# 64 batched 128x128 matrix products: row pairs of a and out packed on 64 partitions

## Chip, cores, metric

One core of one Trainium2 chip. The metric is the device time of one execution in microseconds; lower is better. For this kernel a run is called slow when it is over 1.5% above the fastest of the same kernel; verdicts use the other runs, called fast.

## The reference

```
a, b: (64, 128, 128) float32
out = np.matmul(a, b)              # (64, 128, 128) float32
```

## The kernel before

The first 8 matrices come in as float32 on two hardware queues and are cast by VectorE. All others are cast to float16 while they are loaded, by transfers that GpSimd issues, and the float16 results are cast back to float32 while they are stored, on the same GpSimd queue. TensorE transposes a (against an identity), VectorE copies the transposed block to SBUF, TensorE multiplies, ScalarE evicts.

```
a0f = sb.tile([P, G, P], F32)                  # P = 128, G = 8
nc.sync.dma_start(out=a0f[:, 0:4], in_=a[0:4].rearrange("b m k -> m b k"))
nc.sync.dma_start(out=a0f[:, 4:8], in_=a[4:8].rearrange("b m k -> m b k"))
...                                            # b0f likewise, on the scalar queue
in_chunks = [(8, 16), (16, 32), (32, 48), (48, 64)]
for (lo, hi) in in_chunks:
    sl = ds(lo, hi - lo)
    nc.gpsimd.dma_start(out=a16[:, sl], in_=a[sl].rearrange("b m k -> m b k"))
    nc.gpsimd.dma_start(out=b16[:, sl], in_=b[sl].rearrange("b k n -> k b n"))
...
for g in range(n_groups):                      # 8 groups of 8 matrices
    ...
        nc.tensor.transpose(aT_ps[:, j], a16[:, i], ident)
    nc.vector.tensor_copy(out=aT16[:, gs], in_=aT_ps)
    ...
        nc.tensor.matmul(c_ps[:, j], aT16[:, i], b16[:, i], start=True, stop=True)
    nc.scalar.copy(out=c16[:, gs], in_=c_ps)
    nc.gpsimd.dma_start(out=out[gs].rearrange("b m n -> m b n"), in_=c16[:, gs])
```

## Time and profile before

| | before |
|---|---|
| time, median of 20 runs (range) | 41.75 us (41.54 to 42.31) |
| span of the profiled execution | 40.0 us |
| DMA packets | 24,929 |
| matmul instructions on TensorE | 128 |

A span is shorter than a time by some 1.8 us (41.73 and 40.0 us in the profiled run before, 41.42 and 39.5 after), which lie outside the profile. The prediction reads the steady stretches. Two further places matter for what came of it. The first is the list of DMA queues of the page (packets, MB, time taken as a share of 16 engines' span):

```profile
q0 software_dynamic: 22816, 7.90, 176.9%
q10 hardware_dynamic: 1056, 0.52, 5.0%
q1 hardware_dynamic: 1056, 0.52, 4.7%
q8 instruction: 1, 0.02, 0.1%
```

q0 is GpSimd's queue, q1 and q10 carry the first 8 matrices of a and of b. The last line is one transfer of 16 KB of instructions (the trace has it at 25.1 us, 0.94 us long). The second place is the DMA view of the kernel before from 4 to 5 us, where the first loads are under way and GpSimd's queue has only just begun:

```profile
DMA packets 622, 0.32 MB, mean 318 GB/s; under 512 B 17, under 2 KB 617, under 8 KB 622
q1 hardware_dynamic: 407, 0.20, 73.5%
q10 hardware_dynamic: 207, 0.10, 41.3%
q0 software_dynamic: 8, 0.01, 3.7%
```

At 22.35 ns a row, 622 packets are 13.9 of the 16 us of engine time that this microsecond offers: nearly full.

### The profile page before, as it was taken

The page shows a single profiled execution, that of the slowest core. Times are in us where ns is not written, and L with a number is a line of the kernel's source. Part 1 is how long each engine was busy: PE and PEld are TensorE (multiplying, and loading weights), DVE is VectorE, ACT ScalarE, POOL GpSimd, SP SyncE. Part 2 cuts the span into 40 slices and gives each one's busy share as a digit, 9 for nine tenths or more (in the row PEclk, how much of TensorE's full clock was granted, in tenths as well). Part 3 has the DMA queues.
Part 4 walks back from the last instruction along what each step waited for, and adds up shares of the span by engine and source line. Part 5 has one row for each costly group of instructions (what it writes and reads, how often), then busy time and mean ns, then how long its engine had stood idle before and what let it go on. Part 6 is the DMA issues. An engine that isn't in the chain of part 4 may idle for free.

```text
span 40.0 us, 357 instructions
## 1 busy us (share of the span) xinstructions
PE 12.6 (31%) x128; PEld 10.7 (27%) x128; DVE 7.3 (18%) x12; ACT 9.1 (23%) x9; POOL 16.8 (42%) x21
## 2 busy tenths in 40 slices
PE   0000005085499935007998309004600000000000
PEld 0000013092496904007968208004400000000000
DVE  0000444608400480000076003900000000000000
ACT  0191000000049500900090980000891000000000
POOL 2799999999801780062006279000057400000000
PEclk9999999999999999995557999999655555555555
DMA  0079999999999999999999999999999999999900
GB/s 0 13 210 341 319 247 184 180 179 184 182 180 184 183 180 183 184 179 183 183 181 182 181 182 182 213 362 374 367 365 368 364 363 369 366 360 369 140 9 0
DMA packets 24929, 8.96 MB, mean 224 GB/s; under 512 B 14672, under 2 KB 24912, under 8 KB 24928
## 3 DMA queue, kind: packets, MB, share of 16 engines
q0 software_dynamic: 22816, 7.90, 176.9%
q10 hardware_dynamic: 1056, 0.52, 5.0%
q1 hardware_dynamic: 1056, 0.52, 4.7%
q8 instruction: 1, 0.02, 0.1%
HBM read 8.42 MB, written 4.19 MB: 316 GB/s over the span
## 4 chain that ended last, share of the span: by engine, by line
POOL 38%; issue 36%; POOLq 3%
POOL out_dram L78 15%; POOL a_70 L55 11%; POOL b_71 L56 10%; POOLq L106 2%; POOL ident L50 2%; POOLq L78 0%; POOLq L95 0%
## 5 line engine op out<-in xcount | busy, mean ns | idle before, releaser
L78 POOL DMA_DIRECT2D out_dram<-c_73 x8 | 7.0, 881 | 13.6 <-ACT c_73 L77 13.1
L77 ACT CAST c_73<-c_ps 128x1024 f16<-128x1024 f32 x8 | 7.8, 1014 | 19.1 <-PE c_ps L74 19.1
L70 PE MATMUL aT_ps<-ident,a_70 128*128 128x128 f16 x64 | 7.1, 288 | 11.4 <-DMA ident<-ident_const 6.5
L70 PEld LDWEIGHTS <-a_70 128*128 128x128 f16 x64 | 5.8, 132 | 12.1 <-DMA a_70<-in_a_dram 5.8
L71 DVE COPY aT_72<-aT_ps 128x1024 f16<-128x1024 f16 x8 | 5.3, 689 | 13.0 <-PE aT_ps L70 13.0
L74 PE MATMUL c_ps<-b_71,aT_72 128*128 128x128 f16 x64 | 5.9, 260 | 4.7 <-DMA b_71<-in_b_dram 3.7
L74 PEld LDWEIGHTS <-aT_72 128*128 128x128 f16 x64 | 4.9, 118 | 5.6 <-DVE aT_72 L71 3.0
L56 POOL DMA_DIRECT2D b_71<-in_b_dram x4 | 4.6, 1150 | 0.0
L55 POOL DMA_DIRECT2D a_70<-in_a_dram x4 | 4.5, 1113 | 0.0
L77 ACT ACT_TABLE_LOAD x1 | 1.3, 1283 | 1.8 <-issue 1.8
L58 DVE CAST a_70<-a0f 128x512 f16<-128x512 f32 x1 | 0.6, 561 | 4.5 <-DMA a0f<-in_a_dram 4.5
L50 POOL DMA_DIRECT2D ident<-ident_const x1 | 0.7, 703 | 0.8 <-POOLq L95 0.8
L61 DVE CAST b_71<-b0f 128x512 f16<-128x512 f32 x1 | 0.6, 634 | 0.4 <-DMA b0f<-in_b_dram 0.4
L59 DVE CAST a_70<-a0f 128x512 f16<-128x512 f32 x1 | 0.4, 426 | 0.8 <-DMA a0f<-in_a_dram 0.8
L60 DVE CAST b_71<-b0f 128x512 f16<-128x512 f32 x1 | 0.4, 407 | 0.0
L95 POOL MEMSET const-float32-0.0<- 128x1 f32 x1 | 0.1, 98 | 0.2 <-issue 0.2
L95 POOL MEMSET const-bfloat16-1.0<- 128x1 bf16 x1 | 0.1, 101 | 0.0
L95 POOL MEMSET const-float32-1.0<- 128x1 f32 x1 | 0.1, 98 | 0.0
L95 POOL MEMSET const-uint8-127<- 128x1 uint8 x1 | 0.1, 98 | 0.0
## 6 DMA issues: line engine op xcount, KB each, us to landing
out_dram<-c_73 POOLq DMA_DIRECT2D x8, 512.0 KB, 11.8
a_70<-in_a_dram POOLq DMA_DIRECT2D x3, 512.0 KB, 12.0
b_71<-in_b_dram POOLq DMA_DIRECT2D x3, 512.0 KB, 13.6
b0f<-in_b_dram ACTq DMA_DIRECT2D x2, 256.0 KB, 5.0
a0f<-in_a_dram SPq DMA_DIRECT2D x2, 256.0 KB, 4.4
a_70<-in_a_dram POOLq DMA_DIRECT2D x1, 256.0 KB, 6.1
b_71<-in_b_dram POOLq DMA_DIRECT2D x1, 256.0 KB, 6.7
ident<-ident_const POOLq DMA_DIRECT2D x1, 32.0 KB, 5.2
```

What stands on the lines that cost most here:

```text
L50: nc.gpsimd.dma_start(out=ident, in_=ident_dram.ap())
L55: nc.gpsimd.dma_start(out=a16[:, sl], in_=a[sl].rearrange("b m k -> m b k"))
L56: nc.gpsimd.dma_start(out=b16[:, sl], in_=b[sl].rearrange("b k n -> k b n"))
L58: nc.vector.tensor_copy(out=a16[:, 0:4], in_=a0f[:, 0:4])
L59: nc.vector.tensor_copy(out=a16[:, 4:8], in_=a0f[:, 4:8])
L61: nc.vector.tensor_copy(out=b16[:, 4:8], in_=b0f[:, 4:8])
L70: nc.tensor.transpose(aT_ps[:, j], a16[:, i], ident)
L71: nc.vector.tensor_copy(out=aT16[:, gs], in_=aT_ps)
L74: nc.tensor.matmul(c_ps[:, j], aT16[:, i], b16[:, i], start=True, stop=True)
L77: nc.scalar.copy(out=c16[:, gs], in_=c_ps)
L78: nc.gpsimd.dma_start(out=out[gs].rearrange("b m n -> m b n"), in_=c16[:, gs])
L106: with _tile.TileContext(nc) as tc:
```

## The change

A matrix of a is read as 64 rows of 1 KiB, two neighbouring rows of 512 B each, and lies on 64 partitions; out is stored in the same form. So there are fewer, longer contiguous runs. b stays as it was, since its rows are the contraction. TensorE pays with twice the instructions (256 for 128), ScalarE with 16 evictions on 64 partitions (1010 ns each in the trace after) for 8 on 128 (1014 ns). The split of the loads is changed as well.

```
-    a0f = sb.tile([P, G, P], F32)
+    Fa0f = sb.tile([H, G, 2 * P], F32)                     # H = 64
...
-    nc.sync.dma_start(out=a0f[:, 0:4], in_=a[0:4].rearrange("b m k -> m b k"))
-    nc.sync.dma_start(out=a0f[:, 4:8], in_=a[4:8].rearrange("b m k -> m b k"))
+    nc.sync.dma_start(
+        out=Fa0f, in_=a[0:G].rearrange("b (q two) k -> q b (two k)", two=2)
+    )
...
-    in_chunks = [(8, 16), (16, 32), (32, 48), (48, 64)]
+    in_chunks = [(8, 24), (24, 40), (40, 56), (56, 64)]
...
-            nc.tensor.transpose(aT_ps[:, j], a16[:, i], ident)
+            for e in range(2):
+                nc.tensor.transpose(
+                    aT_ps[:, j, ds(H * e, H)], Fa[:, i, ds(P * e, P)], id64
+                )
...
+        for h in range(G // HG):                            # HG = 4
+            h0 = g0 + h * HG
+            c_ps = ps_c.tile([H, HG, 2 * P], F32)
+            for j in range(HG):
+                i = h0 + j
+                for e in range(2):
+                    nc.tensor.matmul(c_ps[:, j, ds(P * e, P)],
+                        aT16[:, i, ds(H * e, H)], b16[:, i], start=True, stop=True)
+            nc.scalar.copy(out=c16[:, ds(h0, HG)], in_=c_ps)
         nc.gpsimd.dma_start(
-            out=out[gs].rearrange("b m n -> m b n"), in_=c16[:, gs]
+            out=out[gs].rearrange("b (q two) n -> q b (two n)", two=2),
+            in_=c16[:, gs],
         )
```

More of the change, by code (lines that the diff above doesn't have):

```diff
@@ L22 @@
     P = 128
+    H = 64
     B = a.shape[0]
@@ L27 @@
     G = 8
+    HG = 4
     n_groups = B // G
@@ L35 @@
     ident = consts.tile([P, P], F16)
-    a0f = sb.tile([P, G, P], F32)
+    Fa0f = sb.tile([H, G, 2 * P], F32)
     b0f = sb.tile([P, G, P], F32)
-    a16 = sb.tile([P, B, P], F16)
+    Fa = sb.tile([H, B, 2 * P], F16)
     b16 = sb.tile([P, B, P], F16)
     aT16 = sb.tile([P, B, P], F16)
-    c16 = sb.tile([P, B, P], F16)
-    nc.sync.dma_start(out=a0f[:, 0:4], in_=a[0:4].rearrange("b m k -> m b k"))
-    nc.sync.dma_start(out=a0f[:, 4:8], in_=a[4:8].rearrange("b m k -> m b k"))
+    c16 = sb.tile([H, B, 2 * P], F16)
+    nc.sync.dma_start(
+        out=Fa0f, in_=a[0:G].rearrange("b (q two) k -> q b (two k)", two=2)
+    )
     nc.scalar.dma_start(out=b0f[:, 0:4], in_=b[0:4].rearrange("b k n -> k b n"))
@@ L50 @@
     nc.gpsimd.dma_start(out=ident, in_=ident_dram.ap())
-    in_chunks = [(8, 16), (16, 32), (32, 48), (48, 64)]
+    in_chunks = [(8, 24), (24, 40), (40, 56), (56, 64)]
     for (lo, hi) in in_chunks:
         sl = ds(lo, hi - lo)
-        nc.gpsimd.dma_start(out=a16[:, sl], in_=a[sl].rearrange("b m k -> m b k"))
+        nc.gpsimd.dma_start(
+            out=Fa[:, sl],
+            in_=a[sl].rearrange("b (q two) k -> q b (two k)", two=2),
+        )
         nc.gpsimd.dma_start(out=b16[:, sl], in_=b[sl].rearrange("b k n -> k b n"))
-    nc.vector.tensor_copy(out=a16[:, 0:4], in_=a0f[:, 0:4])
-    nc.vector.tensor_copy(out=a16[:, 4:8], in_=a0f[:, 4:8])
+    nc.vector.tensor_copy(out=Fa[:, 0:G], in_=Fa0f)
     nc.vector.tensor_copy(out=b16[:, 0:4], in_=b0f[:, 0:4])
     nc.vector.tensor_copy(out=b16[:, 4:8], in_=b0f[:, 4:8])
+    id64 = ident[0:H, 0:H]
     for g in range(n_groups):
@@ L66 @@
         aT_ps = ps_t.tile([P, G, P], F16)
-        c_ps = ps_c.tile([P, G, P], F32)
         for j in range(G):
             i = g0 + j
-            nc.tensor.transpose(aT_ps[:, j], a16[:, i], ident)
+            for e in range(2):
+                nc.tensor.transpose(
+                    aT_ps[:, j, ds(H * e, H)], Fa[:, i, ds(P * e, P)], id64
+                )
         nc.vector.tensor_copy(out=aT16[:, gs], in_=aT_ps)
-        for j in range(G):
-            i = g0 + j
-            nc.tensor.matmul(
-                c_ps[:, j], aT16[:, i], b16[:, i], start=True, stop=True
-            )
-        nc.scalar.copy(out=c16[:, gs], in_=c_ps)
+        for h in range(G // HG):
[4 more added lines that the diff above has]
+                for e in range(2):
+                    nc.tensor.matmul(
+                        c_ps[:, j, ds(P * e, P)],
+                        aT16[:, i, ds(H * e, H)],
+                        b16[:, i],
+                        start=True,
+                        stop=True,
+                    )
+            nc.scalar.copy(out=c16[:, ds(h0, HG)], in_=c_ps)
         nc.gpsimd.dma_start(
-            out=out[gs].rearrange("b m n -> m b n"), in_=c16[:, gs]
+            out=out[gs].rearrange("b (q two) n -> q b (two n)", two=2),
+            in_=c16[:, gs],
         )
```

## The prediction

> **What bounds the kernel now.** I read the slices of the page first, because the share of the span of each engine is low (PE 31%, ScalarE 23%, VectorE 18%, GpSimd 42%), so none of them is a candidate over the whole.
>
> ```profile
> DMA  0079999999999999999999999999999999999900
> GB/s 0 13 210 341 319 247 184 180 179 184 182 180 184 183 180 183 184 179 183 183 181 182 181 182 182 213 362 374 367 365 368 364 363 369 366 360 369 140 9 0
> DMA packets 24929, 8.96 MB, mean 224 GB/s; under 512 B 14672, under 2 KB 24912, under 8 KB 24928
> ```
>
> A slice is 1.0 us. The 16 DMA engines are at nine tenths from slice 3 to slice 37 without a hole. The rate has two flat levels: about 182 GB/s while inputs are loaded, about 365 GB/s while outputs are stored. That is one level, not two: the size counted is that of the destination. A load reads 512 B of float32 and writes 256 B of float16, a store reads 256 B and writes 512 B. Next I took the DMA view in one stretch of each kind, 10 to 24 us and 27 to 36 us.
>
> ```profile
> DMA packets 10028, 2.55 MB, mean 182 GB/s; under 512 B 10028, under 2 KB 10028, under 8 KB 10028
> ```
>
> ```profile
> DMA packets 6542, 3.29 MB, mean 366 GB/s; under 512 B 108, under 2 KB 6542, under 8 KB 6542
> ```
>
> Loads: 14 us x 16 engines / 10028 packets = 22.3 ns of an engine per packet. Stores: 9 us x 16 / (6542 - 108 small ones) = 22.4 ns. The same time per packet in both directions, whatever side is the float32 one: an engine needs 22.35 ns for a 512 B row, and the kernel is a queue of such rows. Check by adding up: the GpSimd queue carries 56 matrices of a, 56 of b and 64 of c, each 128 rows, 176 x 128 / 16 = 1408 rows per engine, x 22.35 ns = 31.5 us. By the same view its packets start in earnest at 5 us (8 in the slice 4 to 5, 232 in 5 to 6, where the first loads on the other two queues are ending) and end at about 37.3 us. 5.5 + 31.5 = 37.0. So it fits, with no idle in it.
>
> Then the end. The chain of waits follows only GpSimd's issuing and is no help here; the waits of the DMA queue's own engine, SyncE, tell what the end waits for, and the timeline tells when the last stores were queued.
>
> ```profile
> SPq L106 <- DMA out_dram<-c_73: 36.9, 4, 32.8
> ```
>
> ```profile
> 27.47 0.92 PEld L74 LDWEIGHTS <-aT_72 128*128 128x128 f16 x16 [2.58 <-issue]
> 27.50 1.16 PE L74 MATMUL c_ps<-b_71,aT_72 128*128 128x128 f16 x16 [2.44 <-DMA b_71<-in_b_dram]
> 28.14 1.93 ACT L77 CAST c_73<-c_ps 128x1024 f16<-128x1024 f32 x2 [4.27 <-PE c_ps L74]
> 29.45 0.88 POOL L78 DMA_DIRECT2D out_dram<-c_73  x1 [4.41 <-ACT c_73 L77]
> 30.56 0.88 POOL L78 DMA_DIRECT2D out_dram<-c_73  x1 [0.23 <-issue]
> ```
>
> All loads are queued ahead of all stores, so stores start to flow only when the loads end, at 25.6 us (slice 25 is the step in the rate). By then six stores are queued, which last 6 x 64 rows x 22.35 ns = 8.6 us, to 34.2 us. The last store is queued at 31.4 us. Compute is 2.8 us early: it is hidden.
>
> [...]
>
> **The change part by part.**
> *Rows of 1 KiB.* a and out become 64 rows of 1 KiB per matrix; b stays at 512 B. On the GpSimd queue: a 56 x 64 / 16 = 224 rows per engine, out 256, in all 480 rows of 1 KiB in place of 960 of 512 B; b 448 as before. A pair of old rows costs 44.7 ns[...]. I take 1.35 us. All of it is on the path, as the queue has no hole. A page count of about 16,700 packets should result (24,929 - 512 x 16).
> [...]What crosses the SBUF side is float16, half the bytes. [...]I deduct 0.25 us for queueing. Only the first load of a is float32 in SBUF[...]. It runs beside b's first load before the GpSimd queue starts, where the slices 2 to 5 have room (410, 697, 622 and 582 packets against 716 in a full one), so I deduct 0.2 us and not 1.0.
> *TensorE.* 64 transposes and 64 matmuls become 128 and 128. In the timeline 16 of either kind took 1.89 us[...], 1.07 to 1.19 us[...]. 256 instructions: 17 to 19 us, or 30 us. [...] Per group of 8 matrices that is 2.1 to 3.8 us, while loads bring a group in [...]2.8 us. [...] A slow PE may fall behind the loads, but up to the end of the loads it needs only 4 or 5 of the 8 stores ready[...].
> *ScalarE.* 16 evictions of 64x1024 in place of 8 of 128x1024; [...]16 x 1.014 = 16.2 us instead of 7.8. Per group 2.0 us, under the 2.8 us of its loads. *VectorE.* The eight 689 ns copies stay; two casts of a (561 + 426 ns) become one of 64x2048, an estimated 1.2 to 1.6 us by four times the 407 ns of the fastest 512-element one. Off the path.
> *GpSimd.* An issue of 1024 rows takes 0.88 us, of 2048 rows 1.14 to 1.38; 512 rows will take an estimated 0.75. Off the path.
> *Chunks.* (8,24), (24,40), (40,56), (56,64): the last chunk is one group instead of two. After the last b lands, one group is left: 16 matmuls and two evictions, about 2.5 us, as now. The smaller first chunk is lost, at no cost while the queue is full.
> Sum: 1.35 - 0.25 - 0.2 = 0.9 to 1.1 us. 41.79 - 1.1 = 40.7 us.
>
> **The rivals.**
> *A[...].* [...]a row costs more than 44.7 ns. Every ns over that costs 0.48 us. At 48 ns: 43.4 us. [...]
> *B: HBM or bytes bound, not rows.* If 366 GB/s is a byte rate, longer rows do nothing: 41.8 us. For it: loads and stores have the same rate[...]. [...]
> *C: compute turns into the bound.* PE [...]leaves the last stores late. If the last group is done 3 us later than now, at 34.4 us, then the data ends [...]37.3 us: the gain is gone, 41.8 us. For it: the PE count doubles[...]. Against it: 2.8 us of slack now.
>
> **Range and chances.** The main line (40.0 to 40.9 us) gets about half. It is only a little over the 2% line, 40.95 us, so small losses [...]lead to "same", 0.30. Rival A in earnest or C strongly: 0.18 for slower. Range: full gain without deductions and a little luck in the start gives 39.6; a row at 47 ns or a lagging PE gives 43.0.
>
> **What would show it.** Right: some 16,700 packets; in the load stretches alternating rates (a faster than 182 GB/s[...], b at 182); [...]the step from loads to stores near 25 us instead of 25.6; no hole in the DMA row; the last store queued before the DMA has drained the rest. Wrong by A: stores and a's loads below 366 and 182 GB/s. Wrong by B: the same 366 with half the packets. Wrong by C: holes in the DMA row after 25 us, or the last store queued later than about 33.5 us. Also wrong if the start moves: the GpSimd queue begins later than 5 us or the first a lands over 1 us later and group 0 starts late.

The trace before has no row of 1 KiB and no tile on 64 partitions. So the gain of 1.35 us, the 0.25 us, the 0.2 us and the 1.0 us of the first load were the author's estimates and not measured. Rival A is that rows of 1 KiB on 64 partitions cost more than the 44.7 ns of two old ones.

## The result

| | before | after |
|---|---|---|
| median of all runs | 41.75 us (20 runs) | 41.66 us (10 runs; 41.13 to 42.99) |
| ratio of the fast runs | 1 | 0.9902, interval 0.9865 to 0.9938 |
| span of the profiled execution | 40.0 us | 39.5 us |
| DMA packets | 24,929 | 16,722 |

A ratio here and below is the mean time of one kernel's fast runs over that of the other's of the same rounds, so not quite the ratio of the medians. The change gives 1%, 0.41 us of 41.75, where 40.7 us, 1.1 us less, was predicted. With the profiled one, 5 of the changed kernel's 11 runs are slow, at 41.75 to 42.99 us; nothing below is concluded from those.

The slices and queues of the page after:

```profile
DMA  0089999999999999999999999999999999999200
GB/s 0 15 247 283 206 224 223 199 199 181 183 183 196 199 189 183 183 187 199 208 179 182 183 192 188 187 378 397 400 404 403 377 386 403 397 395 299 45 1 0
DMA packets 16722, 8.98 MB, mean 227 GB/s; under 512 B 7488, under 2 KB 16704, under 8 KB 16720
...
q0 software_dynamic: 15136, 7.90, 134.1%
q1 hardware_dynamic: 528, 0.52, 6.1%
q10 hardware_dynamic: 1056, 0.52, 5.8%
q8 instruction: 2, 0.03, 0.3%
```

Three things are to be seen. The rates rose as hoped: a's loads run at 196 to 199 GB/s (slices 7, 8, 12, 13, 18), b's still at 183, the stores at about 400 instead of 365. The start got worse: in slices 3 to 6 the rate is 283, 206, 224, 223, where before it was 341, 319, 247, 184. (The last of before is low because GpSimd's casting loads, which count at 256 B of the 512 B they read, already filled it.) And there are two transfers of instructions instead of one.

The DMA view after, for 12 to 14 us (loads of a) and 27 to 36 us (stores):

```profile
DMA packets 786, 0.40 MB, mean 198 GB/s; under 512 B 17, under 2 KB 786, under 8 KB 786
```

```profile
DMA packets 3573, 3.57 MB, mean 396 GB/s; under 512 B 106, under 2 KB 3572, under 8 KB 3572
```

2 us x 16 / (786 - 17) = 41.6 ns for a 1 KiB row in the loads, 9 us x 16 / (3573 - 106) = 41.5 ns in the stores, the latter with a 16 KB transfer of instructions among them. A pair of old rows took 44.7. So the gain per row is there, in both directions, 3.2 ns: 1.5 us over 480 rows, where the prediction took 1.35. With it the loads of a group come to the 2.8 us of the prediction, 8 x (4 x 41.5 + 8 x 22.35) ns.

The DMA view after from 4 to 5 us, to be held against that of before above:

```profile
DMA packets 230, 0.20 MB, mean 205 GB/s; under 512 B 2, under 2 KB 230, under 8 KB 230
q1 hardware_dynamic: 174, 0.18, 95.1%
q10 hardware_dynamic: 56, 0.03, 17.8%
```

At full rate 174 long rows x 41.5 ns and 56 short ones x 22.35 ns would be 8.5 us of engine time, of 16: with work queued the engines do about half of what they could. A packet of q1 took 87 ns on average (95.1% of 16 us / 174). From 3.5 to 4.5 us, where q1 is almost alone, 201 of its rows start: 206 GB/s. In the half microsecond before, 160 rows of q1 start, 328 GB/s. So this load on partitions 0 to 63 begins fast and then falls to about 206; why is not shown. GpSimd's queue, which had 232 packets in the slice 5 to 6 us before, has 1 there now and 263 in the next.

The last work of the changed kernel in its timeline:

```profile
30.68 0.61 PE L87 MATMUL c_ps<-b_71,aT_72 128*64 128x128 f16 x8 [0.30 <-ACT c_73 L94]
...
30.93 0.69 POOL L95 DMA_DIRECT2D out_dram<-c_73  x1 [1.11 <-ACT c_73 L94]
32.74 0.70 POOL L95 DMA_DIRECT2D out_dram<-c_73  x1 [1.14 <-ACT c_73 L94]
```

The last store is queued at 33.4 us instead of 31.4. The DMA row stays at nine tenths until slice 36, so in this execution compute did not hold the stores, but its lead is mostly used up: the data of the seven stores before it lasted until 35.1 us, 1.6 us longer; by the same measure the lead was 4.4 in the kernel before (35.9 and 31.4).

**Which engine ends last.** GpSimd's queue has 272 packets of 4 bytes for its 17 transfers, so 16 for each, and I take it that every DMA engine ends its share with one of them (the trace does not say which engine a packet is on). Taking these packets in order of time, 16 to a transfer, gives when the median engine and when the late ones were done with it. From the packets of before and after, us (the rows of loads and early stores thinned out):

```
before   median engine done         20.1  23.0  25.9  27.3  30.1  33.0  35.9  37.3
         last engine later by       0.60  0.60  1.09  1.11  1.11  1.11  1.11  1.11
         second last later by       0.42  0.42  0.60  0.60  0.60  0.60  0.60  0.60
         instructions at            25.1
after    median engine done         17.5  20.2  24.4  27.2  29.8  31.1  33.8  36.4
         last engine later by       0.13  1.06  1.06  0.99  1.01  1.03  1.03  1.26
         second last later by       0.13  0.13  0.13  0.13  0.16  0.98  0.98  1.03
         instructions at            19.2, 30.2
```

After each transfer of instructions one engine is some 0.9 us late at once, and in these two traces the lag stays to the end (1.09 to 1.11 us before, 1.06 to 1.26 after). In before the engine that it hit became the last, beside one that was 0.6 us late from the start. So the profiled pair adds up: median engine 37.32 to 36.40 (-0.92), last engine over the median 1.11 to 1.26 (+0.15), last packet to end of span 1.52 to 1.88 (+0.36): -0.41 us in all, the spans' difference. Of two transfers of instructions, then, the last engine shows only 0.15 more than of one.

### The profile page after: what moved, and what is told of

It is laid out like the page before. It is cut to its first block, busy times and chain, and to the rows that moved or that the text cites. A ratio compares the mean times of both kernels' runs of the same rounds, so it can differ in the third digit from the quotient of the medians.

```text
span 39.5 us, 616 instructions
## 1 busy us (share of the span) xinstructions
PE 18.2 (46%) x256; PEld 15.6 (40%) x256; DVE 7.7 (19%) x11; ACT 16.4 (42%) x17; POOL 15.1 (38%) x21
## 2 busy tenths in 40 slices
DMA packets 16722, 8.98 MB, mean 227 GB/s; under 512 B 7488, under 2 KB 16704, under 8 KB 16720
## 4 chain that ended last, share of the span: by engine, by line
issue 46%; POOL 35%; POOLq 2%
POOL out_dram L95 12%; POOL Fa L58 11%; POOL b_71 L62 10%; POOLq L124 2%; POOL ident L53 2%; POOLq L95 0%; POOLq L113 0%
## 5 line engine op out<-in xcount | busy, mean ns | idle before, releaser
L94 ACT CAST c_73<-c_ps 64x1024 f16<-64x1024 f32 x16 | 15.1, 1010 | 14.3 <-PE c_ps L87 14.3
L77 PE MATMUL aT_ps<-ident,Fa 64*128 64x64 f16 x128 | 7.4, 220 | 11.7 <-DVE Fa L64 9.5
L87 PE MATMUL c_ps<-b_71,aT_72 128*64 128x128 f16 x128 | 11.7, 250 | 1.4 <-ACT c_73 L94 1.4
L95 POOL DMA_DIRECT2D out_dram<-c_73 x8 | 5.6, 697 | 17.3 <-ACT c_73 L94 17.3
L77 PEld LDWEIGHTS <-Fa 64*128 64x128 f16 x128 | 6.1, 114 | 12.8 <-DVE Fa L64 9.5
L87 PEld LDWEIGHTS <-aT_72 128*64 128x64 f16 x128 | 9.6, 129 | 2.7 <-issue 2.0
L58 POOL DMA_DIRECT2D Fa<-in_a_dram x4 | 4.4, 1102 | 0.0
L64 DVE CAST Fa<-Fa0f 64x2048 f16<-64x2048 f32 x1 | 1.2, 1203 | 0.0
```

Source lines behind the costliest of these rows:

```text
L58: nc.gpsimd.dma_start(out=Fa[:, sl], in_=a[sl].rearrange("b (q two) k -> q b (two k)", two=2),)
L64: nc.vector.tensor_copy(out=Fa[:, 0:G], in_=Fa0f)
L77: nc.tensor.transpose(aT_ps[:, j, ds(H * e, H)], Fa[:, i, ds(P * e, P)], id64)
L87: nc.tensor.matmul(c_ps[:, j, ds(P * e, P)], aT16[:, i, ds(H * e, H)], b16[:, i], start=True, stop=True,)
L94: nc.scalar.copy(out=c16[:, ds(h0, HG)], in_=c_ps)
L95: nc.gpsimd.dma_start(out=out[gs].rearrange("b (q two) n -> q b (two n)", two=2), in_=c16[:, gs],)
```

## The experiments

All were correct unless said otherwise, and were timed in 5 rounds beside the kernel before on the same chip. Theory P: rows gain as predicted, the float32 load of the first 8 matrices loses on partitions 0 to 63. Theory F: the second transfer of instructions costs too. Rival C: compute holds the stores.

### 1. Undo the start (e1_after_start128)

```
-    Fa0f ... one load of a[0:8] on 64 partitions, 1 KiB rows
+    nc.sync.dma_start(out=a0f[:, 0:4], in_=a[0:4].rearrange("b m k -> m b k"))
+    nc.sync.dma_start(out=a0f[:, 4:8], in_=a[4:8].rearrange("b m k -> m b k"))
...
+            if g == 0:
+                nc.tensor.transpose(aT_ps[:, j], a016[:, i], ident)
...
-                        aT16[:, i, ds(H * e, H)],
+                        aT16[:, i, ds(e, H, step=2)] if g == 0 else aT16[:, i, ds(H * e, H)],
```

> The changed kernel with one part undone: the first 8 matrices of a are loaded as before (two transfers, rows of 512 B, float32 on all 128 partitions); everything else stays packed. Theory P (the changed kernel's start loses about 1 us[...]): the GpSimd queue's packets start near 5.0 us again instead of 6.0, the step from loads to stores moves from 25.7 to about 24.8 us, and the time falls from 41.4 (fast runs of the changed kernel) to about 40.6, ratio to before 0.97. Rival C (compute, that is ScalarE's 16 evictions and the doubled TensorE work, holds the end): the start moves but the last stores are not queued earlier than 32.7 us, holes appear in the stores, and the time stays at 41.2 to 41.5. Rival Q (the GpSimd queue starts late because of its own issues or chunks): the start stays at 6.0 and the time at 41.4.

Measured: ratio 0.9731 (0.9661 to 0.98; 3 of 6 runs fast, 40.37 to 40.84). Undoing the start gains (0.9902 - 0.9731) x 41.75 = 0.7 us. The profiled run is a slow one; only its start is read here, its rates by slice:

```profile
GB/s 0 12 198 332 331 255 191 198 185 180 183 192 198 193 185 183 184 195 199 201 176 183 189 191 183 338 388 395 403 401 395 408 373 390 397 322 74 31 1 0
```

332, 331, 255 in slices 3 to 5: the start of before is back, and the step to the stores comes in slice 25 instead of 26. Theory P expected this; rival Q (GpSimd's own issues or chunks delay its queue) falls, as those are unchanged here.

### 2. The start alone, in short rows (e2_before_start64)

```
+    for e in range(2):
+        nc.sync.dma_start(
+            out=Fa0f[:, e], in_=a[0:G, ds(H * e, H)].rearrange("b q k -> q b k")
+        )
...                                             # group 0: two transposes of 64 rows per matrix
```

> The kernel before with one part of the change alone: the first 8 matrices of a are loaded onto 64 partitions, but in rows of 512 B (rows q and 64 + q instead of pairs of neighbours) and in two transfers. Theory P[...]: the GpSimd queue starts about 0.9 us later than the 5.0 of before, and the time is about 42.6, ratio 1.02, although no row became longer and no transfer was merged. Rival L (the long rows or the single transfer make the late start): start at 5.0 and the time at 41.75.

Measured: ratio 1.0155 (1.0103 to 1.0208), all 6 runs fast: +0.65 us, with rows of 512 B and two transfers as before. So neither the row length nor the merging is needed for a loss; the expected 0.9 was somewhat too much. In its trace the median engine is done with the first GpSimd load at 7.60 us instead of 7.16 and with the last store at 37.83 instead of 37.32; the last engine is 1.48 us late instead of 1.11. So 0.4 to 0.5 us come from the start and the rest from a late engine.

### 3. The merged transfer alone (e7_before_one_dma)

```
+    nc.sync.dma_start(out=a0f, in_=a[0:8].rearrange("b m k -> m b k"))     # in place of two
```

> The kernel before with the first two transfers of a merged to one of 512 KB on 128 partitions, and one cast in place of two. Theory P: start of the GpSimd queue near 5.0, time 41.75, ratio 1.00. Rival L (one transfer instead of two makes the late start): start near 6.0, time 42.6, ratio 1.02.

Measured: 1.0021 (0.9996 to 1.0047). One transfer instead of two costs nothing to speak of.

### 4. 64 other partitions (e11_start64_all_ports)

```
-    Fa0f[:, e]                                  # partitions 0 to 63
+    Fa0f[ds(32, H), e]                          # partitions 32 to 95; cast in pieces of 32
```

> As e2 (the kernel before, first 8 matrices of a on 64 partitions in float32), but on partitions 32 to 95 instead of 0 to 63[...]. Theory P[...]: the loss of e2 goes; GpSimd queue in earnest at 5 to 5.5 us, 41.8, ratio 1.00. Rival N (it is the number of partitions[...]): as e2, 42.4, ratio 1.0155.

Measured: 1.0083 (1.0048 to 1.0118), all 14 runs fast. The DMA view from 3 to 4 us, first of e2, then of this run:

```profile
DMA packets 542, 0.27 MB, mean 271 GB/s; under 512 B 16, under 2 KB 541, under 8 KB 542
```

```profile
DMA packets 696, 0.34 MB, mean 342 GB/s; under 512 B 28, under 2 KB 696, under 8 KB 696
```

The same 64 partitions' worth of data moves at 342 GB/s instead of 271, as in the kernel before (697 packets, 342 GB/s). The line of a's queue in this run, in the same microsecond:

```profile
q1 hardware_dynamic: 518, 0.26, 85.8%
```

Without the 16 small ones that is 257 GB/s into 64 partitions, b's rows beside it. So the rate in the start depends on which 64 partitions are written and not on their number alone; why is not shown. Here too a's first packet comes only at 2.86 us, as in e2 (2.66) and in the changed kernel (2.78; before 1.82), and the first GpSimd load is done at 7.28 us all the same, so that delay is not the cause. The time gives back only 0.3 of the 0.65 us, though: the median engine ends at 37.5 (before 37.3, e2 37.8), but two engines end at 38.75 and 38.98, one late from the start by 1.2 us, the other after the transfer of instructions at 29.0. The expectation of a ratio of 1.00 was missed for this; why an engine is late from the start is open.

### 5. The same rows on 128 partitions (e4_pairs128)

Two neighbouring matrices are 128 row pairs in one piece of memory, so one row pair can go to each of 128 partitions, and a transpose is full-sized again. The two halves of the partitions are the two matrices; each matmul writes the half of PSUM that belongs to its matrix.

```
+    def rows(x):
+        return x.rearrange("(t h) m k -> t (h m) k", h=2).rearrange(
+            "t (p two) k -> p t (two k)", two=2)
...
+        for t in range(G // 2):
+            for e in range(2):
+                nc.tensor.transpose(aT_ps[:, 2*t + e], a16[:, g0//2 + t, ds(P*e, P)], ident)
...
+                    nc.tensor.matmul(c_ps[ds(H*h, H), t, ds(P*e, P)],      # for t, h, e
+                        aT16[:, g0 + 2*t + e, ds(H*h, H)], b16[:, g0 + 2*t + h],
+                        start=True, stop=True)
...
+        nc.gpsimd.dma_start(out=rows(out[gs]), in_=c16[:, ds(g0//2, G//2)])
```

> Another packing with the same 1 KiB rows, on all 128 partitions: one row pair of two neighbouring matrices per partition, so 64 full transposes as before, 128 matmuls of 64 columns whose outputs go to the lower or upper half of the partitions, and 8 evictions of 128 x 1024. Theory P with the row cost (41 ns per 1 KiB against 44.7 for two of 512 B, on 480 rows per engine): rates of 198 and 400 as in the changed kernel, start near 5.0, step near 24.7, time 41.75 - 1.7 = 40.0 to 40.3, ratio 0.96 to 0.965. Rival C (compute holds the changed kernel): same start as e1, but better than e1 by more than 0.4 us. Rival H[...]: a rate above 198 and 400 here.

Measured: 40.28 us, ratio 0.9643 (0.9597 to 0.9689), all 6 runs fast. It is the version that beats both kernels clearly. Its slices:

```profile
DMA  0169999999999999999999999999999999999400
GB/s 0 17 159 336 367 284 174 198 187 183 183 189 197 199 185 183 183 192 198 194 185 183 196 187 186 221 351 401 402 398 401 399 396 395 396 398 307 84 0 0
```

198 in a's loads and 400 in the stores, no more than the changed kernel has on 64 partitions. So rival H, that 64 partitions slow the float16 rows as well, falls at these rates. The start is whole (336, 367, 284). From 4 to 5 us the same 1 KiB float32 rows of a, on 128 partitions, took 44 ns a packet (63.2% of 16 us / 229) where the changed kernel's took 87:

```profile
q1 hardware_dynamic: 229, 0.22, 63.2%
```

The 4-byte packets show the two kernels side by side: the median engine is done with the first GpSimd load of a at 9.10 us in the changed kernel and at 8.20 here, with the last load at 25.85 and 24.97, with the last store at 36.40 and 35.48. The distance is 0.90, 0.88 and 0.92: all of it is there after the start, and nothing is added in 27 us of float16 rows on 64 partitions. The other profiles agree on the first of these times: 9.0 to 9.3 us in the three with the changed kernel's start, 8.2 to 8.4 in the five with long rows and a's first load on all partitions. The last engine is 1.26 us late in the changed kernel and 1.19 here, with a single transfer of instructions.

### 6. Loads alone and stores alone (e13_pairs_loads_only, e14_pairs_stores_only)

```
# loads alone: rows back in order in VectorE's copy, the rest as before
+        nc.vector.tensor_copy(
+            out=aT16[:, gs].rearrange("p (t h) (q e) -> p t (h q) e", h=2, e=2),
+            in_=aT_ps.rearrange("p t e x -> p t x e"))
# stores alone: a as before, output as in 5
+                        aT16[:, i, ds(e, H, step=2)],
```

> The 128-partition packing for the loads of a alone; VectorE's copy out of PSUM puts the rows back in order, and matmuls, evictions and stores are as in the kernel before. 224 rows of 1 KiB per engine x 3.5 ns = 0.78 us less; a rate of 198 in a's loads, 366 in the stores. If the 0.36 us that all kernels with 1 KiB stores lose between the last completion packet and the end belong to the stores, this kernel does not have them: 1.5 to 1.6 us from last packet to end as before, and the time near 41.0, ratio 0.981. If they belong to the packed loads or to the count of TensorE instructions: about 1.88 and ratio near 0.99.

> The 128-partition packing for the stores alone; a is loaded as before, and the matmul takes every second column of the transposed a. 256 rows per engine x 3.5 = 0.90 us less in the stores (400 instead of 366), loads at 182. If the longer end belongs to the 1 KiB stores: 1.88 us from the last packet to the end, so a net 0.54 us, ratio about 0.987. If not: 1.5 to 1.6 us and ratio about 0.979.

Measured: 0.9818 (0.9777 to 0.986) and 0.9767 (0.9736 to 0.9798): -0.76 us for 224 rows per engine and -0.97 us for 256, by the 3.5 ns a row of the expectations, an estimate of the author's, 0.78 and 0.90, by the 3.2 of the trace after 0.72 and 0.82. The gain per row is confirmed by time as well. Both together (run 5) give 1.49, not 1.73. Part of the rest is at the end, which SyncE's waits show, for the kernel before, the changed kernel, loads alone and stores alone:

```profile
SPq L106 <- PEq L106: 0.8, 2, 0.5
```

```profile
SPq L124 <- PEq L124: 1.2, 2, 0.7
```

```profile
SPq L118 <- PEq L118: 0.9, 2, 0.5
```

```profile
SPq L117 <- PEq L117: 1.0, 2, 0.5
```

These are the waits at the closing barrier, after all data has landed. From the last packet to the end it is 1.52, 1.88, 1.61 and 1.69 us, 1.90 in run 5, 1.86 to 1.89 in the other kernels with long rows both ways and 1.51 to 1.62 in those without long rows. Neither half has the 0.36 us alone, so what I asked of these two runs stays unanswered: what makes the closing barrier longer is open. The count of TensorE instructions alone does not (e6 in the next section, 256 pairs: 1.55).

### 7. More instructions on TensorE (e6_before_more_pe, e10_pairs_more_pe)

```
+            for _ in range(3):                  # before; range(2) in the kernel of run 5
                 nc.tensor.transpose(...)
```

> The kernel before with every transpose done three times over (result unchanged): 256 pairs of weight load and matmul, as many as the changed kernel has. Theory F (a second 16 KB transfer of instructions costs the changed kernel part of its gain): two such transfers in the trace, two engines about 1 us late or one 2 us late, and a time 0 to 0.3 us longer with some executions 1 us longer, as the changed kernel has. Rival: nothing but noise, 41.75, no slow executions. A rise above 0.5 us in all executions would speak for TensorE's work itself holding the end.

> The 1 KiB packing on 128 partitions (e4) with every transpose done twice: 256 pairs on TensorE as in the changed kernel, so two 16 KB transfers of instructions instead of one; result and all else unchanged. Theory F (the second transfer is what e1 still lacks against e4): 40.5 to 40.7, near e1's ratio of 0.973, with some slow executions near 41.5. Rival C (the 16 evictions are what e1 lacks): 40.3 as e4.

Measured: 1.0056 (1.0026 to 1.0085; 22 runs) for the first, +0.23 us; 0.9737 (0.967 to 0.9804; 5 of 6 runs fast) for the second against 0.9643 in run 5, +0.39 us. The last queue line of run 5 and of this run:

```profile
q8 instruction: 1, 0.02, 0.2%
```

```profile
q8 instruction: 2, 0.03, 0.3%
```

The first lies in the expected 0 to 0.3 us; the executions 1 us longer did not come (the longest of 22 took 42.71). All six profiles with 248 or more pairs on TensorE have two such transfers, those with 192 or fewer have one (e3's comes after its end). By the same completion packets as above, the lag in e6's trace jumps from 0.45 to 1.5 us after the transfer at 17.0 and the second engine's from 0.37 to 1.18 after the one at 30.1; in e10's from 0.35 to 0.95 after 18.4 and the second's from 0.31 to 0.85 after 30.2. The stores have no hole. At the end the last engine of e6 is 1.46 us late against 1.11 before, which fits theory F and its time. e10 fits less well: its last engine is 1.27 us late, but run 5 had one 1.19 late with a single transfer, and the median engine is 0.18 us slower (35.66 against 35.48), so most of the 0.26 us between their last packets is not this lag. By time, what e1 lacks against run 5 (0.9731 against 0.9643) comes back in e10 with 8 evictions of 128 partitions, so rival C's 16 evictions are not needed for it. But the intervals of e1 and of e10 both overlap that of run 5, the plain mean of e10's five fast runs (40.85 us) would make it 0.55 instead of 0.39, and the repeated transposes are TensorE work as well. Theory F is shown in e6, at 0.23 us with that reserve; for the changed kernel its size stays open.

### 8. Fewer matmuls (e5_before_fewer_pe, e9_after_fewer_pe)

```
# before, wrong on purpose: 32 matmuls of 256 columns
+            nc.tensor.matmul(c_ps[:, ds(j, 2)], aT16[:, i], b16[:, ds(i, 2)], ...)   # even j
# after, wrong on purpose: 64 matmuls of 256 columns
+                nc.tensor.matmul(c_ps[:, j], aT16[:, i, ds(0, H)], b16[:, ds(i - j % 2, 2)], ...)
```

> The kernel before with half of its matmuls (32 of 256 columns each; the result is wrong on purpose, loads, stores, evictions and copies are the same). In the trace of before, a 16 KB transfer of instructions at 25.1 us held one DMA engine for about 1 us, and one engine ended its stores at 38.4 us while 13 of 16 were done by 37.4. Theory F (this transfer is caused by the count of TensorE instructions, about 258, and makes one engine the last): here with about 194 there is no such transfer, the engines end within 0.5 us of each other at about 37.4 to 37.7, and the time is 0.5 to 0.8 us lower, about 41.1, ratio 0.983. Rival: the last engine is slow for another reason; it stays at 38.4 and the time at 41.75.

> The changed kernel with half of its matmuls (64 of 256 columns; wrong result on purpose), transposes and the 16 evictions as they are: 192 pairs on TensorE, so one transfer of instructions, not two. Theory F: the second transfer costs the changed kernel 0.2 to 0.4 us and makes its slow executions; here 41.1 us or a little under, and no execution near 42.5. Rival C (TensorE's doubled work holds the last stores): stores queued earlier and a fall by more than 0.5 us. Rival: no change, 41.35 and the same share of slow executions.

Both gave wrong results, as meant. The first: 0.9857 (0.979 to 0.9924), -0.6 us (the plain means of the fast runs give -0.4), which is about the expected time, but not by the expected way. Its profiled run, a slow one, does have a transfer of instructions, at 31.7 us, and an engine that ends at 38.8. Half the matmuls only put it later. So this run does not show that the transfer sets the end, and why it is faster is open. The second: 2 of 6 runs fast, at 40.84 and 41.11, ratio 0.9752 (0.9655 to 0.9848), one transfer of instructions in its trace; that fits theory F, but a fall of 0.6 us is also what rival C asked for, and two fast runs do not separate them. But four runs are slow, three of them at 43.4 to 43.6, where I expected none near 42.5: the slow executions do not go away with the second transfer. The profiled one is among the slow, and its rates have holes in the stores:

```profile
GB/s 0 34 273 256 195 207 222 196 184 178 183 187 199 197 183 183 184 196 200 197 176 183 193 187 219 378 397 401 403 335 353 201 18 351 154 391 188 407 19 0
```

There the last store is queued at 37.7 us. It suggests that compute can hold the stores in this layout in some executions, and no more; no verdict rests on it.

### 9. Evictions shared (e12_after_split_evict)

```
-            nc.scalar.copy(out=c16[:, ds(h0, HG)], in_=c_ps)
+            if h == 0: nc.scalar.copy(out=c16[:, ds(h0, HG)], in_=c_ps)
+            else:      nc.vector.tensor_copy(out=c16[:, ds(h0, HG)], in_=c_ps)
```

> The changed kernel with every second eviction on VectorE instead of ScalarE, so the 15.1 us of evictions are shared. Rival C (ScalarE's evictions hold the stores in part): last store queued 2 us or more earlier than 32.7, and the fast runs at 41.1 or less. Theory P with F (start and instructions, not evictions): fast runs at 41.2 to 41.5 as in the changed kernel, ratio 0.99.

Inconclusive: one run of 6 is fast, at 41.36, in the range that P with F expects; the other five are slow (42.01 to 42.76), so there is no ratio. An eviction takes 1.22 us on VectorE against 1.00 on ScalarE. Its profiled run, a slow one, queues the last store at 36.3 us and has holes in the stores as e9 has; no verdict rests on that either. It is no improvement in any case.

### 10. The new split of the loads alone (e3_before_chunks)

```
-    in_chunks = [(8, 16), (16, 32), (32, 48), (48, 64)]
+    in_chunks = [(8, 24), (24, 40), (40, 56), (56, 64)]
```

> The kernel before with the new split of the loads alone (8 to 24, 24 to 40, 40 to 56, 56 to 64). All theories here: the queue is full either way, so no effect, 41.8, ratio 0.998 to 1.002. If the split helps or costs over 0.2 us, the sum of the parts has to be told anew.

Measured: 0.9948 (0.9912 to 0.9983) over the 8 fast runs of 22, -0.22 us; but the median of all 22 is 42.0 us against 41.77. The two point in opposite directions, and I read no effect from them. Its profile has no transfer of instructions before the end, and still one engine is 1.3 us late from GpSimd's second transfer on: lags arise in the start too, not only from instructions.

### 11. Rows of 2 KiB (e8_quads128)

```
+    H = 32; R = 4                               # four rows of four matrices per partition
```

> The 128-partition packing taken one step on: four neighbouring rows of four matrices, rows of 2 KiB, 64 transposes and 256 matmuls of 32 columns. Row cost[...]: 240 rows per engine x 3.5 = 0.85 us less than the 1 KiB packing on 128 partitions, about 39.4, ratio 0.944, if compute is hidden. If the 320 pairs on TensorE hold the end or their second transfer of instructions makes an engine late: 40.0 to 40.5.

Measured: 39.34 us once, 40.62 to 40.88 in the other five runs, which are slow by the rule, so no ratio. The stores in the profiled (slow) run:

```profile
GB/s 0 42 210 316 371 231 152 197 185 181 183 192 206 207 184 184 201 188 203 201 183 183 191 198 184 268 394 414 408 408 417 400 410 412 421 378 125 40 0 0
```

The rate rises once more, to about 410 GB/s. (An estimate from the measured rows: each further 512 B adds 41.5 - 22.35 ns, so 2 KiB take 79.8 ns, which would be 411.) So the row cost seems to hold on, though only a slow run shows it. But with 320 pairs on TensorE and two transfers of instructions the time is not steady; run 5 with 40.28 us is the version to use.

## Why the prediction was wrong

- **What bounds the kernel now**: right. It is a queue of rows, and every experiment that shortened the rows' sum moved the time (by 0.76, 0.97 and 1.49 us in e13, e14 and run 5).
- **Rows of 1 KiB**: right in direction and size. 41.5 ns per row instead of 44.7 for two old ones; predicted 1.35 us, an estimate of the author's, measured 0.76 and 0.97 alone and 1.49 together. At the median engine of the traces it is 1.84 (37.32 to 35.48 in run 5), so the 1.35 was rather too little.
- **64 partitions, the step that failed**: "so I deduct 0.2 us and not 1.0" for the first float32 load. The load beside it and the free engine time in slices 2 to 5 were to hide it. They could not: a long row took 87 ns instead of 44, and GpSimd's queue began about a microsecond later. Nor was there much room: by the prediction's own counts slices 3 to 5 lack 19, 94 and 134 packets to a full one, 0.35 us in all, and only slice 2, where the loads are starting, lacks more (306). Measured 0.65 us alone (e2), 0.71 by undoing it (e1), and 0.9 between the traces of the changed kernel and of run 5. That this load would be slower was foreseen; what failed is that it would be hidden. The other half of that step, 0.25 us for queueing of the float16 rows, was not needed: the rates are equal on 64 partitions and on 128 (198 and 400 GB/s).
- **Terms that the sum did not have**: instructions and the end. The doubled TensorE work was judged by its time alone. It also brings a second transfer of 16 KB of instructions, after which one DMA engine is some 0.9 us behind. What that costs is not settled: 0.23 us in e6, 0.39 by the ratio of e10, about 0.1 by the traces of the changed kernel and run 5. And the stretch after the last packet is 0.36 us longer, cause open.
- **The sum**: 1.35 - 0.25 - 0.2 is 0.90, not "0.9 to 1.1", and 40.7 us uses the 1.1 and a time of 41.79 where the median was 41.75. By its own terms it should have said 40.85.
- **Chunks**: no clear effect in e3, as told.
- **Rival A**: false for float16 rows (41.5 ns), and true for the one float32 load (87 ns a row), for which it was not meant. **Rival B** (bytes): false, 400 GB/s. **Rival C** (compute): not in the profiled fast run, where the lead of the last store fell from 4.4 to 1.6 us; two profiled slow runs of this layout (e9, e12) have the last store queued 3 to 4 us later and holes in the stores.
- **What would make it wrong**: "if the start moves: the GpSimd queue begins later than 5 us" was named as such a sign, and is what came.

The sum of the fast runs, in the terms measured: rows -1.49 (run 5), second transfer of instructions +0.39 (e10 against run 5), start +0.71 (e1 against the changed kernel) = -0.39; measured -0.41. The terms come from runs on several chips and each has an interval of some 0.2 us or more, so the sum closing to 0.02 is luck. The +0.4 us at the closing barrier is contained in run 5's 1.49, and its cause is open. So is the cause of the slow executions. The traces divide it otherwise: rows -1.84 and start +0.92 at the median engine, last engine +0.15, closing barrier +0.36, again -0.41, with little left for the second transfer. So the start costs 0.65 to 0.9 us and the second transfer 0.1 to 0.4, and these runs do not tell more.

## What to carry to other kernels

When a layout is changed for longer runs, look at the rate of every transfer on its new partitions, the small first one too: here halving the partitions was free for rows cast to 2 bytes (198 and 400 GB/s, as on 128) and cost 0.65 to 0.9 us for a single 512 KB load in 4 bytes (87 ns a row instead of 44). Look for a layout that has both long rows and all partitions; here two neighbouring matrices gave it, with nothing but another access pattern, and 3.6% instead of 1%. And where the DMA engines are full, count instructions as DMA traffic (after a transfer of 16 KB one engine was some 0.9 us late here): look at the queue of instructions in the page and at the slowest engine, not only at the mean.
